# The last quarter of a feed-forward product as eight plain block products, and seven-product sums moved from GpSimd to VectorE

## The chip, the cores and the metric

The kernel runs on one core of a Trainium2 chip. The core has five engines, each with its own queue of instructions that it works off in order: TensorE (PE in the profile, with its weight loads as PEld), VectorE (DVE), ScalarE (ACT), GpSimd (POOL) and SyncE (SP), which here only issues DMAs. An instruction waits at the head of its queue for semaphores that other engines raise. The metric is the device time of one execution in microseconds (us): the median of three executions.

## The reference

One layer of a decoder block on 512 tokens of width 1024, all in float32. Three token mixers come first (sparse attention, block-sparse attention and a state-space scan), are gated, summed and projected. The change is in what follows them:

```python
h = rms_norm(x, norm2_g[l])
x = x + jnp.square(jax.nn.relu(h @ w_ff1[l])) @ w_ff2[l]      # w_ff1 1024x4096, w_ff2 4096x1024
```

## The kernel before

**Split products.** A float32 product is made of three passes on TensorE. Each operand is split into a high part (ScalarE writes a rounded copy) and a low part (operand minus high part, one subtraction). `mm3` (L358 to L361) issues high x high, high x low and low x high into one PSUM sum. So each operand tile costs one ScalarE activation and one subtraction before TensorE may use it.

**Weights.** `WS` (L120 and on) is a stream of weight blocks of 128x1024 elements. A block is loaded into a raw buffer (`wraw`, 3 buffers, DMA from SP's queue), split into `whi` on ScalarE (L158) and `wlo` on VectorE (L159), 6 buffers of each, and freed when TensorE has used it. `tick` splits up to three blocks past the one in use.

**The feed-forward stage.** The hidden 4096 columns are worked in four quarters q of 1024. `ff_up(q, m)` makes an eighth of a quarter of `h @ w_ff1`: 24 matmuls of 512 columns, then ReLU on ScalarE (L1404) and the square on VectorE (L1405) into tile `f` (`FA[q, half]`). `ff_down(q, i)` is one of the seven products of a fast 2x2 block scheme (seven block products in place of eight, at the price of block sums on both sides): 24 matmuls of 512 columns into two PSUM tiles `sc`, which VectorE then adds into the result `x2` or a partial sum `u2acc` (L1460). Three kinds of extra work belong to the scheme:

- the sums on the weights, in place in the blocks `qd` (L244 to L250), eight per quarter, on VectorE;
- the sums on the activations (L1420 to L1426, tile `fs` or in place in `f`), four per quarter, on GpSimd;
- the low part `fo` of each left operand (L1431), seven per quarter, on GpSimd; its high part `fh` is on ScalarE (L1430). `left(n)` does both, one product ahead.

In quarter 3, after product 2, `u2acc` is added into the three other parts of the result (L1463), one part on VectorE and two on GpSimd, and the parts are sent out as they are finished (L1466).

**Order.** `FSEQ` (L255 to L263) sets the order: the eight `ff_up` of quarter 0, then in each quarter the seven products, with the eight `ff_up` of the next quarter laid between them (1, 2, 1, 1, 1, 2, 0). Quarter 3 has nothing laid between. The tile scheduler then orders each engine's queue, with small moves about that order.

Of the kernel before, what the change touches and what calls it, by code (L numbers as in the profile page):

```python
# [8 lines left out]
F32R = mybir.dt.float32r  # L9
AF = mybir.ActivationFunctionType  # L10
ALU = mybir.AluOpType
# [4 lines left out]
D = 1024  # L16
D_IN = 11512
NB = 4
# [19 lines left out]
def build_kernel(ctx, tc, A, out):  # L38
    nc = tc.nc
    pe, act, dve, pool = nc.tensor, nc.scalar, nc.vector, nc.gpsimd  # L40
    done = set()

    def dram(ap, off, dims):
        return bass.AP(tensor=ap.tensor, offset=ap.offset + off, ap=dims)
# [4 lines left out]
    def f(ap):  # L49
        return ap.bitcast(F32)  # L50
# [3 lines left out]
    def popen(name, side="left", space=None, bufs=1):  # L54
        kw = dict(name=name, bufs=bufs, side=side)
        if space is not None:
            kw["space"] = space
            kw.pop("side")
        cm = tc.tile_pool(**kw)
        p = cm.__enter__()  # L60
        open_pools[name] = cm
        return p
# [26 lines left out]
    def ps(tag, shape, dt=F32, bufs=2):  # L89
        if tag == XT[0]:  # L90
            XT[1] += 1
            if XT[1] % 3 == 0:
                tag = "pF"
        return psp.tile(shape, dt, tag=tag, name=tag, bufs=PSB[tag])
# [88 lines left out]
    ws = WS()  # L183

    def wcols(w, ld, k0, nk, c0, n):
        return dram(w, k0 * 128 * ld + c0, [[ld, 128], [128 * ld, nk], [1, n]])
# [5 lines left out]
    def plan_ch(w, ld, c0, k0=0, nk=8):  # L192
        return ws.add([(wcols(w, ld, k0, nk, c0, 128), 128)], nk, 128)
# [32 lines left out]
    PROD = ("11", "t1", "t2", "t3", "22", "t4", "21")  # L226
    NEEDS = {"11": "11", "t1": "12", "t2": "22", "t4": "21"}

    def quad_block(q, i, s):
        name = PROD[i]  # L230

        def go(loading):
            if loading:
                nm = NEEDS.get(name)
                if nm:
                    t = FL[0].tile([128, 1024], F32, name=f"qd{nm}_{s}")
                    row, col = int(nm[0]) - 1, int(nm[1]) - 1
                    nc.sync.dma_start(t.rearrange("p (a b) -> p a b", b=512),
                                      wcols(A["w_ff2"], D, 8 * q + 4 * row + 2 * s, 2, 512 * col, 512))
                    QD[nm, s] = t  # L240
                return None
            b11, b12, b22, b21 = [QD.get((n, s)) for n in ("11", "12", "22", "21")]
            if name == "t1":
                dve.tensor_tensor(b11, b12, b11, op=ALU.subtract)  # L244
            elif name == "t2":
                dve.tensor_tensor(b11, b22, b11, op=ALU.subtract)
            elif name == "t3":
                dve.tensor_tensor(b12, b22, b12, op=ALU.subtract)
            elif name == "t4":
                dve.tensor_tensor(b11, b21, b11, op=ALU.subtract)  # L250
            return {"t3": b12, "22": b22, "21": b21}.get(name, b11)
        return ws.add(go, 2, 512)

    FL = [None]
    FSEQ = [("F", 0, m) for m in range(8)]  # L255
    for q in range(4):
        m = 0
        for i, nf in enumerate((1, 2, 1, 1, 1, 2, 0)):
            FSEQ.append(("G", q, i))
            for _ in range(nf):  # L260
                if q < 3:
                    FSEQ.append(("F", q + 1, m))
                    m += 1  # L263
    ff = {}
    for kind, q, i in FSEQ:
        if kind == "F":
            ff[kind, q, i] = plan_ch(A["w_ff1"], 4096, q * 1024 + 128 * i)
        else:
            ff[kind, q, i] = [quad_block(q, i, s) for s in range(2)]


    for t in range(1, NB):
# [39 lines left out]
    for t in range(NB):  # L312
# [4 lines left out]
        for k0 in range(0, KT, 4):  # L317
            p = ps("pT", [128, 4, 128])
# [23 lines left out]
    p = ps("pT", [128, 512])  # L342
# [15 lines left out]
    def mm3(o, lh, ll, rh, rl, first, last):  # L358
        pe.matmul(o, lh, rh, start=first, stop=False)  # L359
        pe.matmul(o, lh, rl, start=False, stop=False)  # L360
        pe.matmul(o, ll, rh, start=False, stop=last)  # L361
# [879 lines left out]
    def branches(ya):  # L1241
# [20 lines left out]
        for bi, br in enumerate(BR):  # L1262
# [31 lines left out]
            if br == "b1":  # L1294
# [4 lines left out]
                for half in range(2):  # L1299
                    for m in range(BH):  # L1300
                        wi = P["br_b1"][m]
                        wh, wl = ws.get(wi)
# [5 lines left out]
            for m in range(8):  # L1308
                load_g(8 * bi + m)
                load_g(8 * bi + m + 1)  # L1310
                th = th_.pop(8 * bi + m)
                if br[0] == "c":
                    dve.scalar_tensor_tensor(th, th, 1.0, R, op0=ALU.add, op1=ALU.mult)
                if m in pp:
                    p = pp.pop(m)
                else:
                    p = ps("pj", [128, 512])
# [21 lines left out]
        x2 = fp.tile([128, NB, D], F32, name="x2")  # L1339
# [37 lines left out]
        fl = FL[0] = popen("ffl")  # L1377
        U2 = fl.tile([128, 2, 512], F32, name="u2acc")
        FA = {}
        pp = {}  # L1380
        if NH:
            for m in range(NH):
                pp[m] = ps(("pj", "pj", "sc", "sc")[m], [128, 512])
            for half in range(2):
                cs = slice(256 * half, 256 * half + 256)
                for m in range(NH):
                    wh, wl = ws.get(ff["F", 0, m])
# [6 lines left out]
        def ff_up(q, m):  # L1394
            if m % 4 == 0:
                FA[q, m // 4] = fl.tile([128, 2, 4, 256], F32, name=f"f{m // 4}", bufs=2)
            if q == 0 and m in pp:
                p = pp.pop(m)
            else:
                p = ps("pj", [128, 512])  # L1400
                yield from proj_ch(ff["F", q, m], lambda i: h2h[:, i], lambda i: h2l[:, i], p)
            p2 = p.rearrange("p (a b) -> p a b", a=2)
            fq = FA[q, m // 4][:, :, m % 4]
            act.activation(fq, p2, AF.Relu)  # L1404
            dve.tensor_tensor(fq, fq, fq, op=ALU.mult)  # L1405


        ST, AO = {}, {}

        def left(n):  # L1410
            q, i = divmod(n, 7)
            if q > 3 or n in AO:
                return
            f1 = FA[q, 0]
            a11, a21 = f1[:, 0], f1[:, 1]
            if i not in (0, 3):
                a12, a22 = FA[q, 1][:, 0], FA[q, 1][:, 1]
            if i == 1:
                ST[0] = fl.tile([128, 4, 256], F32, name="fs")
                pool.tensor_tensor(ST[0], a21, a22, op=ALU.add)  # L1420
            elif i == 2:
                pool.tensor_tensor(ST[0], ST[0], a11, op=ALU.subtract)
            elif i == 3:
                pool.tensor_tensor(a21, a11, a21, op=ALU.subtract)
            elif i == 4:
                pool.tensor_tensor(ST[0], a12, ST[0], op=ALU.subtract)  # L1426
            src = a11 if i == 0 else a21 if i == 3 else a22 if i == 5 else a12 if i == 6 else ST[0]
            h_ = fl.tile([128, 4, 256], F32R, name="fh", bufs=2)
            l_ = fl.tile([128, 4, 256], F32R, name="fo", bufs=2)
            act.activation(h_, src, AF.Copy)  # L1430
            pool.tensor_tensor(l_, src, f(h_), op=ALU.subtract)  # L1431
            AO[n] = h_, l_

        def quad(h, n):
            return lambda tt: x2[:, 2 * h + tt, 512 * n:512 * n + 512]

        X11, X12, X21, X22 = quad(0, 0), quad(0, 1), quad(1, 0), quad(1, 1)
        UU = lambda tt: U2[:, tt]
        INTO = ((X11, UU), (X22, X12), (UU,), (X22, X21), (X12,), (X21,), (X11,))
        LAST = {3: (X22, 1, 1), 4: (X12, 0, 1), 5: (X21, 1, 0), 6: (X11, 0, 0)}  # L1440

        def ff_down(q, i):
            ah, al = AO.pop(7 * q + i)
            blk = [ws.get(b) for b in ff["G", q, i]]
            for tt in range(2):
                p = ps("sc", [128, 512])
                for j in range(4):
                    wh, wl = blk[j // 2]
                    cs = slice(128 * tt, 128 * tt + 128)
                    mm3(p, ah[:, j, cs], al[:, j, cs], wh[:, j % 2], wl[:, j % 2], j == 0, j == 3)  # L1450
                    if tt and j % 2:
                        ws.free(ff["G", q, i][j // 2])
                    if tt == 0 and j == 1:
                        left(7 * q + i + 1)
                    yield 3 * 213
                for d in INTO[i]:
                    if q == 0 and i == 0 and d is UU:
                        act.activation(d(tt), p, AF.Copy)
                    else:
                        dve.tensor_tensor(d(tt), d(tt), p, op=ALU.add)  # L1460
                if q == 3 and i == 2:
                    for d in (X22, X12, X21):
                        (dve if d is X22 else pool).tensor_tensor(d(tt), d(tt), UU(tt), op=ALU.add)  # L1463
                if q == 3 and i in LAST:
                    d, h, n = LAST[i]
                    nc.sync.dma_start(dram(out, (2 * h + tt) * 128 * D + n * 512, [[D, 128], [1, 512]]), d(tt))  # L1466

        for kind, q, i in FSEQ:
            if kind == "F":
                yield from ff_up(q, i)  # L1470
                if q == 0 and i == 5:
                    left(0)
            else:
                yield from ff_down(q, i)
        pclose("ffl")
        pclose("ff")

# [82 lines left out]
```

## Time and profile before

| what | value |
|---|---|
| median of three executions | 1436.81 us (1435.62 to 1438.63) |
| the profiled execution | 1434.21 us, its span in the trace 1432.5 us |
| PE busy | 1364.9 us, 95% of the span |
| DVE busy | 1089.1 us, 76% |
| ACT busy | 722.5 us, 50% |
| POOL busy | 482.4 us, 34% |
| feed-forward stage | about 1099 us to the end of the span |
| last quarter's products | from about 1377 us to the end |

Busy time of PE is time in which at least one matmul is under way; matmuls overlap, so what a matmul costs is read from the distance between two starts, not from its own duration. The profiled execution is 2.60 us under the median of the three, and its span leaves 1.71 us outside.

### The profile page before, as it was taken

What the parts mean: (1) busy time and instruction counts of PE and PEld (TensorE: products, weight loads), DVE (VectorE), ACT (ScalarE), POOL (GpSimd) and SP (SyncE); (2) the same over time, 40 slices, a digit from 0 to 9 for tenths busy, and PEclk for the clock granted to TensorE, in tenths of its full rate; (3) what the DMA queues carried; (4) which work ended last, traced back from release to release, by engine and by line L of the source; (5) the groups of instructions that cost most, each with busy time, mean ns of one, the idle gap of its engine ahead of it and who ended that gap; (6) DMA issues with size and microseconds to landing.
All of it is one profiled execution on the core that took longest, in us unless ns stands there. A gap on an engine that the chain in (4) does not pass through costs nothing.

```text
span 1432.5 us, 19782 instructions
## 1 busy us (share of the span) xinstructions
PE 1364.9 (95%) x6736; PEld 1121.9 (78%) x6736; DVE 1089.1 (76%) x1944; ACT 722.5 (50%) x1442; POOL 482.4 (34%) x342
## 2 busy tenths in 40 slices
PE   6989799999999989999999999999799999999988
PEld 5878688888887767888888777787589888888866
DVE  4599966898977555488568897888655797979796
ACT  5545236667665675555555555545324444444442
POOL 5455211101056676111013524424000342526265
PEclk9999899999999999999999999999899999999999
DMA  6336464453586688843337743424555232331401
GB/s 202 81 96 139 126 205 126 136 133 103 139 229 200 202 230 218 229 141 107 89 94 208 207 129 100 117 65 131 178 184 172 79 118 89 106 115 53 136 4 59
DMA packets 232098, 195.93 MB, mean 137 GB/s; under 512 B 17200, under 2 KB 183484, under 8 KB 231996
## 3 DMA queue, kind: packets, MB, share of 16 engines
q1 hardware_dynamic: 226524, 183.12, 44.3%
q0 software_dynamic: 4608, 8.39, 2.2%
q10 hardware_dynamic: 864, 3.15, 0.6%
q8 instruction: 53, 0.87, 0.3%
q14 instruction: 49, 0.40, 0.1%
HBM read 157.85 MB, written 36.77 MB: 136 GB/s over the span
## 4 chain that ended last, share of the span: by engine, by line
PE 70%; DVE 14%; DMA 7%; issue 4%; ACT 3%; POOL 2%; SPq 1%; DVEq 0%; POOLq 0%; ACTq 0%
PE pj L359 16%; PE pj L360 16%; PE pj L361 15%; PE sc L359 3%; PE sc L361 3%; PE sc L360 3%; PE pT L831 2%; DVE wlo L159 2%; PE sc L796 2%; PE sc L795 2%; PE pv L844 2%; PE pv L843 1%; DMA gld<-g_d 1%; DVE mask L766 1%; DMA E<-ac_d 1%
## 5 line engine op out<-in xcount | busy, mean ns | idle before, releaser
L158 ACT ACTIVATE whi<-wraw 128x1024 fp32r<-128x1024 f32 (+3 forms) x180 | 173.2, 971 | 176.3 <-PE pj L360 115.7
L159 DVE TENSOR_TENSOR wlo<-wraw,whi 128x1024 fp32r<-128x1024 f32 (+1 forms) x156 | 192.9, 1238 | 60.3 <-ACT whi L158 59.2
L359 PE MATMUL pj<-hTh,whi 128*128 128x512 f32 x384 | 154.9, 403 | 0.4 <-DVE cacc L726 0.4
L361 PE MATMUL pj<-hTh,wlo 128*128 128x512 f32 x384 | 153.6, 400 | 0.0
L360 PE MATMUL pj<-hTl,whi 128*128 128x512 f32 x384 | 153.3, 399 | 0.0
L359 PE MATMUL pj<-whi,hTh 128*128 128x512 f32 (+2 forms) x352 | 141.6, 404 | 8.3 <-DVE stk L429 3.1
L804 ACT ACTIVATE p<-p,nb,rs 128x256 f32<-128x256 f32 (+3 forms) x192 | 123.2, 645 | 52.0 <-DVE nb L802 52.0
L360 PE MATMUL pj<-wlo,hTh 128*128 128x512 f32 (+2 forms) x352 | 139.6, 397 | 0.1
L361 PE MATMUL pj<-whi,hTl 128*128 128x512 f32 (+2 forms) x352 | 138.3, 393 | 0.0
L159 DVE TENSOR_TENSOR wlo<-qd,whi 128x1024 fp32r<-128x1024 f32 x56 | 101.3, 1815 | 25.6 <-ACT whi L158 25.6
L359 PE MATMUL pj<-yh,whi 128*128 128x512 f32 x256 | 103.6, 409 | 9.8 <-ACT yh L709 8.2
L815 POOL TENSOR_TENSOR p<-p,rc 128x256 f32<-128x256 f32 (+3 forms) x48 | 38.2, 796 | 220.7 <-DVE rc L810 67.1
L158 ACT ACTIVATE whi<-qd 128x1024 fp32r<-128x1024 f32 x56 | 58.9, 1055 | 87.6 <-PE sc L361 38.9
L360 PE MATMUL pj<-yl,whi 128*128 128x512 f32 x256 | 102.6, 401 | 0.3 <-DVE yl L710 0.3
L361 PE MATMUL pj<-yh,wlo 128*128 128x512 f32 x256 | 102.3, 400 | 0.0
L359 PE MATMUL sc<-whi,fh 128*128 128x512 f32 x224 | 88.9, 397 | 8.2 <-DVE u2acc L1460 4.8
L360 PE MATMUL pj<-h2l,whi 128*128 128x512 f32 (+1 forms) x256 | 96.3, 376 | 0.0
L361 PE MATMUL pj<-h2h,wlo 128*128 128x512 f32 (+1 forms) x256 | 96.2, 376 | 0.0
L359 PE MATMUL pj<-h2h,whi 128*128 128x512 f32 (+1 forms) x256 | 96.1, 376 | 0.0
L360 PE MATMUL sc<-wlo,fh 128*128 128x512 f32 x224 | 88.6, 396 | 0.0
L361 PE MATMUL sc<-whi,fo 128*128 128x512 f32 x224 | 88.3, 395 | 0.0
L359 PEld LDWEIGHTS pj<-whi,hTh 128*128 128x128 f32 x352 | 68.2, 194 | 22.4 <-issue 6.6
(349 smaller groups left out, 3476.3 us busy)
## 6 DMA issues: line engine op xcount, KB each, us to landing
wraw<-in_w_in_dram SPq DMA_DIRECT2D x84, 512.0 KB, 4.4
wraw<-in_w_ff_dram SPq DMA_DIRECT2D x32, 512.0 KB, 4.3
qd<-in_w_ff_dram SPq DMA_DIRECT2D x32, 512.0 KB, 4.7
gld<-g_d SPq DMA_DIRECT2D x48, 256.0 KB, 3.2
q_d<-qev SPq DMA_DIRECT2D x128, 64.0 KB, 2.7
qu<-q_d POOLq DMA_DIRECT2D x32, 256.0 KB, 3.6
E<-ac_d SPq DMA_DIRECT2D x16, 512.0 KB, 4.9
wraw<-in_w_br_ssd_dram SPq DMA_DIRECT2D x16, 512.0 KB, 4.0
```

The lines of the kernel that those rows point to most:

```text
L158: act.activation(hi[:, :m], r[:, :m], AF.Copy)
L159: (pool if i < NP else dve).tensor_tensor(lo[:, :m], r[:, :m], f(hi[:, :m]), op=ALU.subtract)
L359: pe.matmul(o, lh, rh, start=first, stop=False)
L360: pe.matmul(o, lh, rl, start=False, stop=False)
L361: pe.matmul(o, ll, rh, start=False, stop=last)
L766: dve.scalar_tensor_tensor(wk, r[:, :n], iwt[:, b, h:h + 1], caus[:, 384 - 128 * b:] if h == 0 else wk, op0=ALU.mult, op1=ALU.add)
L795: pe.matmul(s_[:, h % w, :n], u.q[:, h], kh[:, :n], start=True, stop=False)
L796: pe.matmul(s_[:, h % w, :n], u.q[:, h], kl[:, :n], start=False, stop=True)
L804: act.activation(u.p[h][:, :n], u.p[h][:, :n], AF.Exp, bias=u.nb[:, h:h + 1], scale=rs8[:, u.b, u.h0 + h:u.h0 + h + 1], accum_out=u.sm[:, ...
L815: pool.tensor_tensor(u.p[h][:, :n], u.p[h][:, :n], bc(rc[:, h:h + 1], [128, n]), op=ALU.mult)
L831: pe.transpose(pt[:, h], u.p[h][:, kb * 128:kb * 128 + 128], ident)
L844: pe.matmul(o, vk, pl0, start=False, stop=en)
```

## The change

Two things. First, the sums on the activations, the low parts `fo`, and the additions of `u2acc` run on VectorE; GpSimd has no work left in the feed-forward stage. Second, quarter 3 is no longer seven products with sums but two plain products `ff_last(o)`, one for each half of the 1024 output columns: eight weight blocks `plain_block`, split in the ordinary way, four token tiles each of 24 matmuls in one PSUM sum `pj`. The left operands are the four quarters of `f` with no sums, `gh` and `gl` (high and low), made once and kept; they take the buffers of the weight blocks `qd` of the same shape. The additions of `u2acc` into the other parts move to quarter 2.

```diff
+    def plain_block(q, o, s):
+        ws_parts = [(wcols(A["w_ff2"], D, 8 * q + 2 * s, 2, 512 * o, 512), 512)]
+        return ws.add(ws_parts, 2, 512)
...
-    for q in range(4):
+    for q in range(3):
...
             for _ in range(nf):
-                if q < 3:
-                    FSEQ.append(("F", q + 1, m))
-                    m += 1
+                FSEQ.append(("F", q + 1, m))
+                m += 1
+    FSEQ += [("H", 3, 0), ("H", 3, 1)]
...
+        def ff_last(o):
+            if o == 0:
+                for nm, kh, th in (("12", 0, 0), ("22", 0, 1), ("11", 1, 0), ("21", 1, 1)):
+                    src = FA[3, kh][:, th]
+                    h_ = fl.tile([128, 4, 256], F32R, name=f"gh{nm}", tag=f"qd{nm}_0")
+                    l_ = fl.tile([128, 4, 256], F32R, name=f"gl{nm}", tag=f"qd{nm}_1")
+                    act.activation(h_, src, AF.Copy)
+                    dve.tensor_tensor(l_, src, f(h_), op=ALU.subtract)
+                    AO[kh, th] = h_, l_
+            idx = ff["H", 3, o]
+            for t in range(NB):
+                p = ps("pj", [128, 512])
+                cs = slice(128 * (t % 2), 128 * (t % 2) + 128)
+                for s in range(4):
+                    wh, wl = ws.get(idx[s])
+                    ah, al = AO[s // 2, t // 2]
+                    for k2 in range(2):
+                        j = 2 * (s % 2) + k2
+                        mm3(p, ah[:, j, cs], al[:, j, cs], wh[:, k2], wl[:, k2], s == 0 and k2 == 0, s == 3 and k2 == 1)
+                    if t == NB - 1:
+                        ws.free(idx[s])
+                    yield 6 * 213
+                x2s = x2[:, t, o * 512:o * 512 + 512]
+                dve.tensor_tensor(x2s, x2s, p, op=ALU.add)
+                nc.sync.dma_start(dram(out, t * 128 * D + o * 512, [[D, 128], [1, 512]]), x2s)
...
-                pool.tensor_tensor(ST[0], a21, a22, op=ALU.add)
+                dve.tensor_tensor(ST[0], a21, a22, op=ALU.add)
...
-            pool.tensor_tensor(l_, src, f(h_), op=ALU.subtract)
+            dve.tensor_tensor(l_, src, f(h_), op=ALU.subtract)
...
-                if q == 3 and i == 2:
+                if q == 2 and i == 2:
                     for d in (X22, X12, X21):
-                        (dve if d is X22 else pool).tensor_tensor(d(tt), d(tt), UU(tt), op=ALU.add)
-                if q == 3 and i in LAST:
-                    d, h, n = LAST[i]
-                    nc.sync.dma_start(dram(out, (2 * h + tt) * 128 * D + n * 512, [[D, 128], [1, 512]]), d(tt))
+                        dve.tensor_tensor(d(tt), d(tt), UU(tt), op=ALU.add)
```

The other three sums of `left` move from `pool` to `dve` in the same way. The order of every engine is the same before and after up to the feed-forward stage.

The first place is VectorE at the opening of quarter 2's products (about 1293 us in the trace of before). `f_12138` and `f_12407` are the two halves of quarter 2's activations, `qd` the weight blocks, `x` the result. Before:

```order
L246 TENSOR_TENSOR qd_0_12526<-qd_0_12726,qd_0_12526 128x1024
L1460 TENSOR_TENSOR x_10770<-x_10770,sc 128x512
L159 TENSOR_TENSOR wlo<-qd_1_12565,whi 128x1024
L1460 TENSOR_TENSOR x_10770<-x_10770,sc 128x512
L159 TENSOR_TENSOR wlo<-wraw,whi 128x1024
L246 TENSOR_TENSOR qd_1_12565<-qd_1_12758,qd_1_12565 128x1024
L1460 TENSOR_TENSOR x_10770<-x_10770,sc 128x512
```

After:

```order
L250 TENSOR_TENSOR qd_0_12526<-qd_0_12726,qd_0_12526 128x1024
L1491 TENSOR_TENSOR x_10770<-x_10770,sc 128x512
L1452 TENSOR_TENSOR fs<-f_12138,f_12407 128x1024
L159 TENSOR_TENSOR wlo<-qd_1_12565,whi 128x1024
L1491 TENSOR_TENSOR x_10770<-x_10770,sc 128x512
L1456 TENSOR_TENSOR f_12138<-f_12138 128x1024
L159 TENSOR_TENSOR wlo<-wraw,whi 128x1024
L250 TENSOR_TENSOR qd_1_12565<-qd_1_12758,qd_1_12565 128x1024
L1463 TENSOR_TENSOR fo<-fs,fh 128x1024
L1491 TENSOR_TENSOR x_10770<-x_10770,sc 128x512
```

Two sums and one low part, which stood in GpSimd's queue, now stand in VectorE's between the same seven instructions.

The second place is VectorE at the passage from quarter 2 to quarter 3 (about 1372 us). Before, the queue goes on with weight differences and low parts of `qd` blocks:

```order
L1405 TENSOR_TENSOR f_12988<-f_12988 128x2x256
L246 TENSOR_TENSOR qd_1_13146<-qd_1_13256,qd_1_13146 128x1024
L1460 TENSOR_TENSOR x_10770<-x_10770,sc 128x512
L159 TENSOR_TENSOR wlo<-qd_0_13107,whi 128x1024
L1460 TENSOR_TENSOR x_10770<-x_10770,sc 128x512
L159 TENSOR_TENSOR wlo<-qd_1_13146,whi 128x1024
L250 TENSOR_TENSOR qd_0_13107<-qd_0_13354,qd_0_13107 128x1024
L1460 TENSOR_TENSOR x_10770<-x_10770,sc 128x512
L1460 TENSOR_TENSOR u2acc<-u2acc,sc 128x512
```

After, with `gl` the low parts of quarter 3's activations, this is the rest of VectorE's queue to the end of the program:

```order
L159 TENSOR_TENSOR wlo<-wraw,whi 128x1024
L1411 TENSOR_TENSOR f_12994<-f_12994 128x2x256
L1491 TENSOR_TENSOR x_10770<-x_10770,sc 128x512
L1420 TENSOR_TENSOR gl_13262<-f_12994,gh_13261 128x1024
L1420 TENSOR_TENSOR gl_13266<-f_12994,gh_13265 128x1024
L1491 TENSOR_TENSOR x_10770<-x_10770,sc 128x512
L159 TENSOR_TENSOR wlo<-wraw,whi 128x1024 x2
L1436 TENSOR_TENSOR x_10770<-x_10770,pj 128x512 x3
L159 TENSOR_TENSOR wlo<-wraw,whi 128x1024 x2
L1436 TENSOR_TENSOR x_10770<-x_10770,pj 128x512 x5
```

What remains there is two low parts of activations, five of weights and eight additions of finished sums into the result.

## Rows read from the trace of the kernel before

**Rows 1.** Busy time by stretch: window, length, then PE, PEld, DVE, ACT, POOL busy (instructions), clock, DMA.
```profile
1254.00:1336.00 82.00, 82.00 (x364) 67.89 (x363) 69.32 (x59) 33.77 (x37) 31.66 (x11) 1.00 0.34 104
...
1372.00:1432.50 60.50, 48.60 (x194) 37.62 (x192) 47.25 (x41) 18.08 (x18) 39.00 (x14) 0.94 0.10 35
```

**Rows 2.** Waits of PE from 1099 us on: who for whom, total us, times, longest.
```profile
PE sc L359 <- DVE u2acc L1460: 4.8, 2, 4.3
...
PE sc L359 <- DVE x L1460: 3.4, 3, 2.7
```

**Rows 3.** Timeline of PE: start, us, engine, line, instruction [idle before, releaser].
```profile
1308.24 0.39 PE L359 MATMUL sc<-whi,fh 128*128 128x512 f32 x1
...
1363.77 0.39 PE L361 MATMUL pj<-h2h,wlo 128*128 128x512 f32 x1
...
1371.93 0.39 PE L361 MATMUL pj<-h2h,wlo 128*128 128x512 f32 x1
1372.16 0.39 PE L359 MATMUL sc<-whi,fh 128*128 128x512 f32 x1
...
1387.57 0.63 PE L359 MATMUL sc<-whi,fh 128*128 128x512 f32 x1 [4.31 <-DVE u2acc L1460]
1388.00 0.63 PE L360 MATMUL sc<-wlo,fh 128*128 128x512 f32 x1
...
1410.60 0.47 PE L359 MATMUL sc<-whi,fh 128*128 128x512 f32 x1 [2.70 <-DVE x L1460]
...
1428.42 0.39 PE L361 MATMUL sc<-whi,fo 128*128 128x512 f32 x1
```

**Rows 4.** Timeline of POOL, opening of quarter 2's products and of quarter 3's.
```profile
1300.21 3.37 POOL L1431 TENSOR_TENSOR fo<-fs,fh 128x1024 fp32r<-128x1024 f32 x1
...
1381.81 3.34 POOL L1431 TENSOR_TENSOR fo<-fs,fh 128x1024 fp32r<-128x1024 f32 x1
```

**Rows 5.** Timeline of DVE, the same two places and the last addition.
```profile
1286.53 1.21 DVE L244 TENSOR_TENSOR qd<-qd,qd 128x1024 f32<-128x1024 f32 x1
1287.66 1.21 DVE L159 TENSOR_TENSOR wlo<-wraw,whi 128x1024 fp32r<-128x1024 f32 x1
...
1293.42 1.22 DVE L246 TENSOR_TENSOR qd<-qd,qd 128x1024 f32<-128x1024 f32 x1
...
1301.26 3.42 DVE L246 TENSOR_TENSOR qd<-qd,qd 128x1024 f32<-128x1024 f32 x1
1304.59 0.68 DVE L1460 TENSOR_TENSOR x<-x,sc 128x512 f32<-128x512 f32 x1
1305.19 0.67 DVE L1460 TENSOR_TENSOR u2acc<-u2acc,sc 128x512 f32<-128x512 f32 x1
...
1382.86 3.37 DVE L250 TENSOR_TENSOR qd<-qd,qd 128x1024 f32<-128x1024 f32 x1
...
1428.84 0.69 DVE L1460 TENSOR_TENSOR x<-x,sc 128x512 f32<-128x512 f32 x1 [2.03 <-PE sc L361]
```

**Rows 6.** DVE by groups from 1372 us on: count, busy us, mean ns, idle before.
```profile
L159 DVE TENSOR_TENSOR wlo<-qd,whi 128x1024 fp32r<-128x1024 f32 x11 | 24.2, 2200 | 0.8 <-ACT whi L158 0.8
```

**Rows 7.** Timeline of ACT, opening of quarter 2's products and the passage to quarter 3.
```profile
1294.89 1.06 ACT L158 ACTIVATE whi<-qd 128x1024 fp32r<-128x1024 f32 x1 [2.76 <-issue]
1296.25 1.06 ACT L158 ACTIVATE whi<-wraw 128x1024 fp32r<-128x1024 f32 x1 [0.29 <-PE sc L361]
1297.21 1.05 ACT L1430 ACTIVATE fh<-fs 128x1024 fp32r<-128x1024 f32 x1
...
1372.18 1.06 ACT L158 ACTIVATE whi<-qd 128x1024 fp32r<-128x1024 f32 x1 [3.89 <-PE pj L360]
1373.14 0.58 ACT L1404 ACTIVATE f<-pj 128x512 f32<-128x512 f32 x1
```

**Rows 8.** DMA issues by line: count, size each, median us to landing.
```profile
qd<-in_w_ff_dram SPq DMA_DIRECT2D x32, 512.0 KB, 4.7
```

**Rows 9.** Busy time of the opening of quarter 2's products, columns as in rows 1.
```profile
1293.42:1321.14 27.72, 27.72 (x124) 22.95 (x123) 26.97 (x20) 12.21 (x13) 22.04 (x7) 1.00 0.14 38
```

More of the change, by code (lines that the diff above doesn't have):

```diff
@@ L267, in build_kernel @@
             ff[kind, q, i] = plan_ch(A["w_ff1"], 4096, q * 1024 + 128 * i)
+        elif kind == "G":
+            ff[kind, q, i] = [quad_block(q, i, s) for s in range(2)]
         else:
-            ff[kind, q, i] = [quad_block(q, i, s) for s in range(2)]
+            ff[kind, q, i] = [plain_block(q, i, s) for s in range(4)]
     for t in range(1, NB):
@@ L1411, in left @@
             q, i = divmod(n, 7)
-            if q > 3 or n in AO:
+            if q > 2 or n in AO:
                 return
@@ L1419, in left @@
                 ST[0] = fl.tile([128, 4, 256], F32, name="fs")
-                pool.tensor_tensor(ST[0], a21, a22, op=ALU.add)
+                dve.tensor_tensor(ST[0], a21, a22, op=ALU.add)
             elif i == 2:
-                pool.tensor_tensor(ST[0], ST[0], a11, op=ALU.subtract)
+                dve.tensor_tensor(ST[0], ST[0], a11, op=ALU.subtract)
             elif i == 3:
-                pool.tensor_tensor(a21, a11, a21, op=ALU.subtract)
+                dve.tensor_tensor(a21, a11, a21, op=ALU.subtract)
             elif i == 4:
-                pool.tensor_tensor(ST[0], a12, ST[0], op=ALU.subtract)
+                dve.tensor_tensor(ST[0], a12, ST[0], op=ALU.subtract)
             src = a11 if i == 0 else a21 if i == 3 else a22 if i == 5 else a12 if i == 6 else ST[0]
@@ L1439, in branches @@
         INTO = ((X11, UU), (X22, X12), (UU,), (X22, X21), (X12,), (X21,), (X11,))
-        LAST = {3: (X22, 1, 1), 4: (X12, 0, 1), 5: (X21, 1, 0), 6: (X11, 0, 0)}
         def ff_down(q, i):
@@ L1472, in branches @@
                     left(0)
+            elif kind == "G":
+                yield from ff_down(q, i)
             else:
-                yield from ff_down(q, i)
+                yield from ff_last(i)
         pclose("ffl")
```

## The prediction

> **What bounds the kernel now.** I read the busy time by stretch first. In quarter 2's stretch TensorE is busy for all of 82.00 us at clock 1.00; in the last 60.50 us it is busy for 48.60 us and the clock is 0.94 [rows 1]. So the feed-forward stage has two parts with different limits. The waits of TensorE confirm it: from 1099 us on it has five waits that count, all before products `sc`, all on VectorE's additions, 8.2 us together [rows 2], and the timeline of TensorE puts them in quarter 3 [rows 3]. Before that, TensorE alone sets the time, and nothing done on VectorE or GpSimd can make it shorter, only longer.
>
> What a matmul of 512 columns costs at full clock is the distance of two starts: 1363.77 to 1371.93 us is 36 of them, 0.2267 us each [rows 3]. From 1372.16 us (first matmul of the last product of quarter 2) to the last matmul at 1428.42 us there are 192 matmuls, 24 of that product and 7 x 24 of quarter 3. Their starts would span 191 x 0.2267 = 43.30 us; they span 56.26 us. So **quarter 3 loses 12.96 us** on TensorE. Part of it is waiting (one wait alone is 4.31 us), part the slow clock behind a wait: after the wait that ends at 1387.57 the distance is 0.43 us, the 1.2 GHz level [rows 3].
>
> Why only there: in quarters 0 to 2 the eight `ff_up` blocks, 8 x 24 x 0.2267 = 43.5 us of TensorE, lie between the products and give VectorE and GpSimd time. In quarter 3 there are none, while each product still wants its weight sums, weight lows and additions on VectorE and its sum and low part on GpSimd, one after the other.
>
> A second thing is in the rows. A VectorE operation with 1024 columns and both inputs in SBUF takes 1.21 us, start to start 1.13 us, when GpSimd is quiet (1286.53 to 1287.66), and 3.42 or 3.37 us when GpSimd is at work (1301.26 beside the low part of 1300.21; 1382.86 beside that of 1381.81). The additions from PSUM, 512 columns, take 0.68 us beside either, 0.60 start to start [rows 4, 5]. In quarter 3 the weight lows average 2.20 us [rows 6]. **Each of the two engines slows the other**, and GpSimd's own operation takes 3.3 to 3.4 us.
>
> **The change, part by part.**
>
> *Quarter 3's matmuls.* Seven products of 24 become eight blocks' worth: two halves x four token tiles x 24 = 192 matmuls for 168. TensorE gets 24 x 0.2267 = **5.44 us more work**. Shapes and operand types are the same, so the same price holds.
>
> *Quarter 3's side work.* Gone are 8 weight sums, 6 of 14 weight splits, the 4 activation sums, 3 of 7 activation splits, and of 20 additions into `x2` and `u2acc` all but 8. What is left at the passage is short. The last `ff_up` ends at 1372.16. ScalarE makes one weight high part (to 1373.24) and the last ReLU (to 1373.72) [rows 7]; VectorE the low part of that block (about 1374.5), the square (0.68, about 1375.1); then ScalarE the two high parts `gh` (1.06 each, start to start about 1.0 [rows 7]: to 1377.2), and VectorE an addition and the two `gl` (1.21 each: the first at about 1377.4, the second 1378.6). TensorE is meanwhile in the last product of quarter 2, until 1372.16 + 24 x 0.2267 = 1377.60, and the first plain sum starts with 12 matmuls on the other half of the activations, done long before. `gh` and `gl` are first wanted at 1377.60 + 2.72 = 1380.32: **2.7 us or more to spare**, and the scheduler has also put matmuls of the next sum there. If the cover fails, the delay is what exceeds 2.7 us.
>
> *Its weights.* Blocks 0 to 3 take the places in the split buffers that the first blocks of quarter 3 take now, so they are split as early as those. Blocks 6 and 7 take the buffers of blocks 0 and 1, free after the 78th and 84th matmul, at 1395.3 and 1396.6; a high and a low part are 1.06 + 1.21, so both are there by about 1399.2, and the second half starts at 1377.60 + 96 x 0.2267 = 1399.36 and wants block 6 at its 13th matmul, 1402.1. Bytes loaded are the same, eight blocks of 512 KB. I take nothing for this; the bound is one late block, its load of 4.7 us [rows 8] + 1.06 + 1.21 = 7 us once.
>
> *Its outputs.* Eight as before, the last after the last addition. The tail from the last matmul's start to the end of the span is 1432.5 - 1428.42 = 4.08 us and stays.
>
> *Sums and lows on VectorE in quarters 0 to 2.* Eleven operations per quarter move, 11 x 1.13 = 12.4 us. VectorE is busy 69.32 of 82 us there, but at the long durations. At the quiet ones a quarter has 22 weight lows and 8 weight sums (30 x 1.13) and 8 squares and 20 additions (28 x 0.60): 50.7 us, with the eleven 63.1, 77% of 82. The opening of a quarter's products is the dense place: VectorE is busy 26.97 of 27.72 us [rows 9]. That is 9 operations of 1024 columns and 9 of 512 whole; the new order puts 6 more of 1024 into the same piece. At quiet prices 15 x 1.13 + 9 x 0.60 = 22.4 us: it fits, with 5.3 us over.
>
> Now the waits that this adds: a low part now waits at the head of VectorE's queue for ScalarE's `fh`, and behind it stand the additions that free PSUM and the next weight lows, for which TensorE waits. I follow the second piece of the order from 1293.42 [rows 5]: weight sum, addition (1294.55), activation sum (1295.15), weight low (1296.28; its high part is there at 1295.95), addition (1297.42), activation sum (1298.02), weight low (1299.15; high part at 1297.31), weight sum (1300.29), low part `fo` (1301.42; `fh` was done at 1298.26 in the order of now) to 1302.63; the times of the high parts are in [rows 7]. On GpSimd it ended at 1300.21 + 3.37 = 1303.58 [rows 4], and TensorE starts that product at 1308.24 [rows 3]. So the low part comes about 1 us **earlier** than now, and 5.6 us before its product. I take nothing for the quarters' openings, with 0 to some 2 us each as the bound.
>
> *The six additions of `u2acc` in quarter 2.* Three of 512 columns, 3 x 0.60 = 1.8 us, twice, about 1326 and 1332 us. Behind them stand weight lows of the product after next, and an `ff_up` (5.4 us) lies between each two products there. Nothing for the sum; 1.8 us each if the cover were gone.
>
> VectorE's 1024-column operations take 1.21 us beside a quiet GpSimd and 3.37 us beside a busy one [rows 5]. A rule of the Trainium skill speaks against the move: Trace Analysis, section Optimizing Scalar/DVE Operations, says that where VectorE is saturated it may make sense to give work to ScalarE or even GpSimd, and here work is given back to it. The same paragraph adds that the two share an SBUF read port, so that moving work between them might not help, and SBUF — State Buffer, section Who interferes with whom, says that a VectorE instruction with two SBUF inputs contends with a GpSimd instruction that reads SBUF. By the first sentence alone the openings overflow (the third rival's sum); by the second the 3.37 us go back to 1.21. The trace agrees with the second: 1.21 against 3.37 us.
>
> *Sum.* From 1372.16 there are 24 + 192 = 216 matmuls without a wait; the last starts at 1372.16 + 215 x 0.2267 = 1420.90, 7.52 us earlier than 1428.42. (12.96 of loss gone, 5.44 of work added.) The profiled execution was 1434.21, so 1426.69 in its terms; it lies 2.60 under the median of the three, 1436.81. Against that median: 1436.81 - 7.5 = **1429.3 us**.
>
> **The rivals.**
>
> 1. *A smaller gain*: openings and passage cost TensorE 1 to 4 us in all, since the scheduler's order was made for other durations and VectorE holds more in one queue. For it: the dense stretch [rows 9] and the one queue. Against: 5 us to spare where I followed it. 1430.3 to 1433.3.
>
> 2. *The change doesn't remove the wait but moves it to the weights*: one plain block is late at the head of a half, 7 us once. For it: the plain stage runs through four blocks in its first 24 matmuls, 5.4 us, where a product used two. Against: the blocks ahead of it are split while TensorE is in earlier work. 1429.3 + 7 = 1436.3, no change.
>
> 3. *VectorE becomes the bound, and it is slower*: the long durations do not come from GpSimd, but from something that stays, such as ScalarE or the DMAs. Then the opening of each quarter gets six more operations of 2.20 us [rows 6], 13.2 us on top of 26.97 in 27.72 us; 12.5 over, less some 5 us of slack before the product that waits, 7.5 us each, three times: 1429.3 + 22 = 1452 us. It decides from the mean duration at which 15 x d + 9 x 0.60 fills 27.72 us: d = 1.49 us. Against it: every long row that I saw lies beside a GpSimd row, and the quiet 1.21 us rows have ScalarE and DMA at work beside them.
>
> **How the numbers follow.** Forecast 0.80; rival 1 0.09; rival 2 0.06; rival 3 0.05. A difference of 0.2%, 2.9 us, is about what a measurement of this kernel can tell from no change. The forecast and nearly all of rival 1 lie beyond it: faster 0.88, same 0.07, slower 0.05. The range takes the forecast with the spread of the three runs (1.2 below their median, 1.8 above), some more below for that median's own error, and rival 1 but for its end: 1426.8 to 1432.8.
>
> **What would show it.** TensorE at clock 1.00 and without a wait over 1 us from 1099 us to the end; 192 matmuls into `pj` in some 43.5 us, the last starting near 1420.9; VectorE's 1024-column operations all near 1.2 us in the stage, its busy time per quarter near 63 us; GpSimd empty. Wrong would be: waits of TensorE on `fo`, `wlo` or on additions at about 1140, 1215 or 1297 us (rivals 1 and 3), on `whi` or a load at about 1378 or 1400 us (rival 2), or 1024-column operations over 1.5 us with GpSimd idle (rival 3).

## The result

The changed kernel takes **1427.97 us**, median of 5 runs (1425.82 to 1431.64); the kernel before, run beside it, 1438.56 us (5 runs, 1435.62 to 1441.98). The ratio on record is **0.9948, with a 95% interval of 0.9927 to 0.9969**: faster by 0.5%. It is not the quotient of these two medians, which is 0.9926; e0 below, against 18 runs of the kernel before, has 0.9948 too. The forecast was 1429.3 us in a range of 1426.8 to 1432.8.

The profiled execution took 1425.82 us with a span of 1424.1 us. Busy time of the page of after, share of the span and number of instructions for each engine:

```profile
PE 1365.5 (96%) x6760; PEld 1126.1 (79%) x6760; DVE 1044.6 (73%) x1959; ACT 712.6 (50%) x1433; POOL 347.0 (24%) x294
```

Busy time of after by stretch, columns as in [rows 1]; the second line is the stretch of quarter 2, the third the last part of the kernel, the fourth the opening of quarter 2's products as in [rows 9]:

```profile
1172.00:1254.00 82.00, 82.00 (x364) 67.89 (x363) 64.98 (x71) 33.74 (x37) 0.00 (x0) 1.00 0.34 103
1254.00:1336.00 82.00, 82.00 (x364) 67.89 (x363) 68.60 (x76) 33.75 (x37) 0.00 (x0) 1.00 0.26 77
1372.00:1424.10 52.10, 48.44 (x214) 39.79 (x212) 15.70 (x18) 6.87 (x8) 0.00 (x0) 0.99 0.17 61
1293.42:1321.14 27.72, 27.72 (x124) 22.96 (x123) 27.20 (x30) 12.19 (x13) 0.00 (x0) 1.00 0.20 57
```

GpSimd (the last busy column) is empty. From 1372 us on VectorE has 18 operations instead of 41, and the clock is 0.99 instead of 0.94. The waits of TensorE from 1095 us on had two groups that counted [rows 2]; after, that view has no row at all.

TensorE's timeline of after, at the places of [rows 3]: start, duration, engine, line, instruction.

```profile
1307.86 0.39 PE L365 MATMUL sc<-whi,fh 128*128 128x512 f32 x1
...
1371.32 0.39 PE L365 MATMUL sc<-whi,fh 128*128 128x512 f32 x1
...
1376.76 0.39 PE L365 MATMUL pj<-whi,gh 128*128 128x512 f32 x1
...
1420.06 0.39 PE L367 MATMUL pj<-whi,gl 128*128 128x512 f32 x1
```

The second and the last row are what the forecast was made of: from the first matmul of quarter 2's last product to the last matmul of the kernel, 1371.32 to 1420.06, it takes **48.74 us** where it took 56.26. The forecast's sum says 215 x 0.2267 = 48.74. Of the 8.4 us by which the profiled span became shorter (1432.5 to 1424.1), 7.5 are these; 0.84 come from ahead of the change: the first matmul of the last stage's `ff_up` starts at 1085.39 instead of 1086.23, in code that is the same in both. That matmul in the two timelines, before and after:

```profile
1086.23 0.28 PE L359 MATMUL pj<-h2h,whi 128*128 128x256 f32 x1
```

```profile
1085.39 0.28 PE L365 MATMUL pj<-h2h,whi 128*128 128x256 f32 x1
```

### The profile page after: what moved, and what is told of

It is laid out like the page before. It is cut to its first block, busy times and chain, and to the rows that moved or that the text cites. A ratio compares the mean times of both kernels' runs of the same rounds, so it can differ in the third digit from the quotient of the medians.

```text
span 1424.1 us, 19720 instructions
## 1 busy us (share of the span) xinstructions
PE 1365.5 (96%) x6760; PEld 1126.1 (79%) x6760; DVE 1044.6 (73%) x1959; ACT 712.6 (50%) x1433; POOL 347.0 (24%) x294
## 4 chain that ended last, share of the span: by engine, by line
PE 71%; DVE 10%; DMA 7%; issue 4%; ACT 4%; POOL 2%; SPq 2%; DVEq 0%; ACTq 0%; POOLq 0%
PE pj L365 17%; PE pj L366 17%; PE pj L367 16%; PE sc L366 3%; PE sc L367 3%; PE sc L365 3%; PE pT L837 2%; PE sc L802 2%; PE sc L801 2%; PE pv L850 2%; PE pv L849 2%; DVE wlo L159 1%; DMA gld<-g_d 1%; SPq L525 1%; DMA E<-ac_d 1%
## 5 line engine op out<-in xcount | busy, mean ns | idle before, releaser
L158 ACT ACTIVATE whi<-wraw 128x1024 fp32r<-128x1024 f32 (+3 forms) x188 | 181.7, 975 | 210.8 <-PE pj L366 124.3
L365 PEld LDWEIGHTS pj<-hTh,whi 128*128 128x128 f32 x384 | 72.3, 188 | 16.4 <-issue 1.7
L367 PEld LDWEIGHTS pj<-hTh,wlo 128*128 128x128 f32 x384 | 72.2, 188 | 15.2 <-issue 1.2
L366 PEld LDWEIGHTS pj<-hTl,whi 128*128 128x128 f32 x384 | 72.3, 188 | 15.0 <-issue 1.7
L841 ACT ACTIVATE pth<-pT 128x512 fp32r<-128x512 f32 x95 | 55.0, 593 | 56.8 <-PE pT L837 54.8
L366 PEld LDWEIGHTS pj<-wlo,hTh 128*128 128x128 f32 x352 | 68.4, 194 | 14.9 <-issue 2.2
```

Of the source, the lines that this page charges most:

```text
L158: act.activation(hi[:, :m], r[:, :m], AF.Copy)
L841: act.activation(ph, ptf, AF.Copy)
```

## The experiments

Since the part ahead of the feed-forward stage does not take the same time twice, I compare two stretches inside the profiled execution: **A**, from the first `ff_up` matmul (`pj` from `h2h`) to the first matmul of quarter 2's last product; and **B**, from there to the last matmul. Before: A 285.93 us, B 56.26 us. B is 43.30 us for seven products without any loss and 48.74 us for eight blocks. A and B are read from one profiled execution of each kernel; e3 to e7 also have one run each, so their whole times tell little.

| kernel | first `ff_up` starts at | A | B | loss in B | time, us (runs) |
|---|---|---|---|---|---|
| before | 1086.23 | 285.93 | 56.26 | 12.96 | 1438.56 (5) |
| the change | 1085.39 | 285.93 | 48.74 | 0.0 | 1427.97 (5) |
| e0_change | 1085.17 | 285.93 | 48.73 | 0.0 | 1427.35 (6) |
| e1_plain_only | 1082.11 | 285.93 | 48.73 | 0.0 | 1427.10 (7) |
| e2_move_only | 1087.79 | 285.93 | 54.76 | 11.46 | 1433.83 (12) |
| e3_lows_twice | 1086.96 | 285.93 | 48.73 | 0.0 | 1427.4 (1) |
| e4_lows_four | 1086.69 | 309.62 | 48.73 | 0.0 | 1450.82 (1) |
| e5_24_fewer | 1093.75 | 285.93 | 43.30 | 0.0 | 1428.74 (1) |
| e6_fewer_adds | 1088.84 | 285.93 | 47.68 | 4.38 | 1428.26 (1) |
| e7_four_psum | 1092.23 | 285.93 | 51.90 | 8.60 | 1435.83 (1) |

e0, e1, e2 and e5 ran on one chip, where the kernel before took 1435.35 us (18 runs); e3, e4, e6 and e7 on another, 1434.82 us (1 run).

### Which part of the change does it: e0, e1, e2

**e0_change** is the changed kernel again, for the comparison on one chip.

> The changed kernel again, beside the others of this call. Theory: 0.9948 of the kernel before, about 7.5 us less, from quarter 3 alone; from the last product of quarter 2 on, 216 matmuls of 0.2267 us without a wait, the last start 48.7 us after the first.

Measured: 1427.35 us, ratio 0.9948 (0.9928 to 0.9968), B 48.73 us.

**e1_plain_only** keeps the plain quarter 3 and puts the sums and low halves of the activations back on GpSimd (one line of five shown):

```diff
-            dve.tensor_tensor(l_, src, f(h_), op=ALU.subtract)
+            pool.tensor_tensor(l_, src, f(h_), op=ALU.subtract)
```

> Only one part of the change: quarter 3 as plain products, but the sums and low parts of quarters 0 to 2 stay on GpSimd. Theory (TensorE is the bound in quarters 0 to 2 whatever the other two engines do, and the plain products alone end quarter 3's waits): 7.5 us less than before, no wait of TensorE from 1099 us on, while VectorE's operations with 1024 columns still take 2 to 3.4 us beside GpSimd. Rival (the gain needs the move to VectorE, since the slow operations hold up the passage to quarter 3): less than 4 us gained, with waits of TensorE at about 1297 or 1377 us.

Measured: 1427.10 us, ratio 0.9952 (0.9933 to 0.9970), B 48.73 us, A 285.93 us, and no wait row of TensorE from 1095 us on. **The plain quarter 3 alone is the whole gain.** The move is worth nothing in quarters 0 to 2, though it does change VectorE's durations. Groups of VectorE from 1172 to 1372 us (count, busy us, mean ns of one, idle before them), first after, then e1:

```profile
L159 DVE TENSOR_TENSOR wlo<-qd,whi 128x1024 fp32r<-128x1024 f32 x32 | 38.9, 1221 | 18.5 <-ACT whi L158 18.5
L159 DVE TENSOR_TENSOR wlo<-wraw,whi 128x1024 fp32r<-128x1024 f32 x22 | 26.9, 1224 | 24.6 <-ACT whi L158 24.6
L1491 DVE TENSOR_TENSOR x<-x,sc 128x512 f32<-128x512 f32 x40 | 26.5, 682 | 0.2
```

```profile
L159 DVE TENSOR_TENSOR wlo<-qd,whi 128x1024 fp32r<-128x1024 f32 x32 | 56.6, 1779 | 16.3 <-ACT whi L158 16.3
L159 DVE TENSOR_TENSOR wlo<-wraw,whi 128x1024 fp32r<-128x1024 f32 x22 | 32.1, 1457 | 18.1 <-ACT whi L158 18.1
L1491 DVE TENSOR_TENSOR x<-x,sc 128x512 f32<-128x512 f32 x39 | 25.8, 679 | 0.2
```

With GpSimd at work the low parts of the summed weight blocks take 1.78 us on average, without it 1.22; the additions from PSUM take 0.68 us either way. These are the durations that the Trainium skill (SBUF — State Buffer, section Who interferes with whom) would lead one to look for: it says that a VectorE instruction contends with a reading GpSimd instruction when both its inputs lie in SBUF, and not with at most one there, outside VectorE's two-port modes; the trace agrees. But all of it is hidden behind TensorE, which is busy for the whole of both stretches.

**e2_move_only** is the kernel before, with seven products in quarter 3, and everything that GpSimd did in this stage on VectorE:

```diff
-            pool.tensor_tensor(l_, src, f(h_), op=ALU.subtract)
+            dve.tensor_tensor(l_, src, f(h_), op=ALU.subtract)
...
-                        (dve if d is X22 else pool).tensor_tensor(d(tt), d(tt), UU(tt), op=ALU.add)
+                        dve.tensor_tensor(d(tt), d(tt), UU(tt), op=ALU.add)
```

> Only the other part: the sums, low parts and additions of the partial sum on VectorE, quarter 3 still as seven products. At quiet prices VectorE has from 1372 us on 25 operations of 1.13 us and 29 of 0.60 us, 45.7 us, against 43.3 us of TensorE for its 192 matmuls. Theory (the two engines slow each other, so quarter 3's loss is mostly their collision): the loss of 12.96 us falls to 3 to 6 us, 7 to 10 us less than before, as good as the whole change. Rival (the one queue of VectorE is as slow as the two engines side by side, and only the plain products help): the loss stays over 10 us, less than 3 us gained.

Measured: 1433.83 us, ratio 0.9991 (0.9976 to 1.0005), B 54.76 us: a loss of 11.46 us where my theory had 3 to 6. The whole time does not differ from the kernel before beyond its interval. **My theory fell**, and the rival was right: one queue of VectorE with all the work is nearly as slow as the two engines side by side. TensorE's waits of e2 from 1095 us on:

```profile
PE sc L359 <- DVE u2acc L1460: 3.5, 2, 2.4
PE sc L359 <- DVE x L1460: 3.1, 1, 3.1
PE sc L361 <- DVE fo L1431: 0.3, 1, 0.3
```

VectorE's timeline of e2 in quarter 3:

```profile
1383.46 1.22 DVE L250 TENSOR_TENSOR qd<-qd,qd 128x1024 f32<-128x1024 f32 x1
1384.59 1.22 DVE L1431 TENSOR_TENSOR fo<-fs,fh 128x1024 fp32r<-128x1024 f32 x1
...
1413.03 1.22 DVE L159 TENSOR_TENSOR wlo<-qd,whi 128x1024 fp32r<-128x1024 f32 x1
1414.16 1.35 DVE L1460 TENSOR_TENSOR x<-x,sc 128x512 f32<-128x512 f32 x2
1418.03 0.69 DVE L1460 TENSOR_TENSOR x<-x,sc 128x512 f32<-128x512 f32 x1 [2.52 <-PE sc L361]
```

Busy time of e2 from 1373.72 us, where B starts, to 1415.50, and over the whole of B; then over B in the kernel before (columns as in [rows 1]):

```profile
1373.72:1415.50 41.78, 34.79 (x135) 26.79 (x134) 41.23 (x48) 16.79 (x17) 0.00 (x0) 0.92 0.04 13
1373.72:1428.48 54.76, 47.77 (x192) 37.49 (x191) 45.22 (x53) 17.85 (x18) 0.00 (x0) 0.94 0.09 34
```

```profile
1372.16:1428.42 56.26, 48.05 (x193) 37.49 (x191) 46.40 (x40) 18.08 (x18) 39.00 (x14) 0.94 0.09 33
```

The durations are the quiet ones, 1.22 us where they were 3.37 [rows 5], and yet VectorE is busy for 41.23 of 41.78 us. Over B it is busy 45.22 us with 53 operations, against 46.40 us with 40 operations before: the operations that came from GpSimd took up what the shorter durations gave. VectorE is the bound of this stretch in both kernels. Only after 1415.50 does it wait for TensorE, and there more than two products are still to be multiplied, 12.98 us up to 1428.48.

This does not show that the two engines cost each other little in the kernel before. There, two groups of VectorE hold the long operations of quarter 3, the low parts of [rows 6] and two weight sums (from 1372.16 us on):

```profile
L250 DVE TENSOR_TENSOR qd<-qd,qd 128x1024 f32<-128x1024 f32 x2 | 5.5, 2775 | 0.0
```

At 1.21 us each the two groups would take 24.2 - 13.3 = 10.9 and 5.5 - 2.4 = 3.1 us less, 14.0 us of VectorE's time. The move takes these away, and brings ten operations of 1.13 us and four of 0.60 us into B, 13.7 us. By this estimate it is an even trade. A run without the collision and without the added work was not made.

The trace of before also shows what the collision is. From 1099 us on, 37 of the 38 VectorE operations of 1024 columns that took over 1.3 us (rows of one operation alone) end 1.08 to 1.10 us after the GpSimd operation that was running when they began, whether they began early in it or late; the 38th ran beside two GpSimd additions that the trace merges into one row. So VectorE's operation in effect waits until GpSimd's is done. In [rows 4, 5] GpSimd is done at 1385.15 and VectorE at 1386.23. GpSimd's next operation is done at 1388.44, and VectorE's, though it began 2.12 us into it, at 1389.53. The last row is a GpSimd operation with VectorE idle for most of it; it takes 2.40 us where the one of [rows 4] beside VectorE's takes 3.34.

```profile
1385.23 3.21 POOL L1422 TENSOR_TENSOR fs<-fs,f 128x1024 f32<-128x1024 f32 x1
```

```profile
1387.35 2.18 DVE L250 TENSOR_TENSOR qd<-qd,qd 128x1024 f32<-128x1024 f32 x1
```

```profile
1418.94 2.40 POOL L1431 TENSOR_TENSOR fo<-f,fh 128x1024 fp32r<-128x1024 f32 x1 [3.99 <-ACT fh L1430]
```

### What kind of limit quarter 3 had: e6, e7

Both start from e2. **e6_fewer_adds** leaves out additions of quarter 3:

```diff
-                for d in INTO[i]:
+                for d in (INTO[i][:1] if q == 3 else INTO[i]):
...
-                if q == 3 and i == 2:
+                if q == 3 and i == 2 and False:
```

> The move alone (quarter 3 as seven products, all side work on VectorE), with 12 additions of quarter 3 left out, so that part of the result is missing: the second target of the three products that have two, and the six additions of the partial sum. They stand in VectorE's queue but prepare no operand: 12 x 0.60 = 7.2 us. From the first matmul of quarter 2's last product to the last matmul it was 54.76 us with them, 11.46 over the 43.30 of TensorE. Theory (quarter 3 is held by the amount of work in VectorE's one queue): 47 to 50 us. Rival (it is held by the chain sum, high part, low part, product, whose length the additions do not change): 53 us or more.

Measured: B 47.68 us. 12 additions of 0.60 us, 7.2 us of VectorE's queue, take **7.08 us** off the end, and the rival's 53 us is not reached. So in e2 it is in the main the sum of what stands in VectorE's queue that set quarter 3's end, not one chain of dependent steps. Busy time of e6 over B, and VectorE's last weight low part:

```profile
1374.77:1422.45 47.68, 44.47 (x192) 35.46 (x191) 38.11 (x41) 17.85 (x18) 0.00 (x0) 1.00 0.11 39
```

```profile
1409.16 1.22 DVE L159 TENSOR_TENSOR wlo<-qd,whi 128x1024 fp32r<-128x1024 f32 x1
```

The two figures agree more closely than their parts. That low part starts 39.31 us after the start of B in e2 and 34.39 us in e6, 4.92 us sooner; the other 2.16 us lie behind it, and TensorE's clock over B is 1.00 here and 0.94 in e2. Six of the twelve additions also read a PSUM buffer, which comes free sooner without them; e6 does not part this from the queue.

**e7_four_psum** gives quarter 3's products four PSUM buffers instead of two:

```diff
-                p = ps("sc", [128, 512])
+                p = ps("pj" if q == 3 and i % 2 else "sc", [128, 512])
```

> The move alone, with quarter 3's products in turn in the two PSUM buffers `sc` and the two of `pj` that lie idle there, so that TensorE need not wait for an addition before the next product. TensorE's waits in the move alone are named after these additions. Theory (the queue of VectorE is what is full, the PSUM wait only where it shows): 52 us or more from the first matmul of quarter 2's last product to the last, little under the 54.76. Rival (two PSUM buffers are too few): 48 us or less, a version that beats the change.

Measured: B 51.90 us, 2.86 us of the 11.46 won, between the two bounds that were set for it: a little under the theory's 52 us, far over the rival's 48. TensorE's waits of e7 from 1095 us on:

```profile
PE sc L359 <- ACT fh L1430: 2.1, 1, 2.1
PE sc L361 <- DVE fo L1431: 1.5, 1, 1.5
PE pj L359 <- DVE x L1460: 1.5, 1, 1.5
```

The waits for additions are shorter, and waits for the activations' halves have come in their place: a part of the loss was buffers. That the rest is VectorE's queue fits e2 and e6, but e7 does not show it by itself. Of the versions with seven products and all their additions this is the best, and it still needs 3.17 us more for B than eight plain blocks.

### Is TensorE the bound now: e5

**e5_24_fewer** leaves 24 of the 192 matmuls of quarter 3 out, the number by which eight blocks exceed seven products:

```diff
-                    for k2 in range(2):
+                    for k2 in range(1 if s == 3 else 2):
```

> The change with 24 of the 192 matmuls of the plain products left out (the last eighth of the inner dimension of each sum), so that part of the result is not computed. Theory (TensorE sets the end, 0.2267 us a matmul): from the first matmul of quarter 2's last product to the last matmul 191 x 0.2267 = 43.3 us, 5.4 us less than the change. Rival (weights, loads or VectorE set the pace of the plain stage): less than 3 us shorter, with waits of TensorE in its place.

Measured: B 43.30 us, which is 5.43 us less: 24 x 0.2267 = 5.44. TensorE alone sets the end of the changed kernel, and the price of the added work is what the forecast took. The whole time, 1428.74 us, shows nothing of that: in this execution the first `ff_up` started 8.4 us later than in the change, ahead of everything edited. TensorE's timeline of e5:

```profile
1379.68 0.39 PE L365 MATMUL sc<-whi,fh 128*128 128x512 f32 x1
```

```profile
1422.98 0.39 PE L367 MATMUL pj<-whi,gl 128*128 128x512 f32 x1
```

### How much room VectorE has in quarters 0 to 2: e3, e4

The changed kernel, with each low half of quarters 0 to 2's products made two and four times over (7 and 21 operations more in each quarter):

```diff
-            dve.tensor_tensor(l_, src, f(h_), op=ALU.subtract)
+            for _ in range(2):
+                dve.tensor_tensor(l_, src, f(h_), op=ALU.subtract)
```

> The change with the low part of each left operand of quarters 0 to 2 made twice on VectorE, the same result written again: 7 more operations of 1.13 us per quarter, 2 or 3 of them in the dense opening. Theory (the opening fits with 5.3 us over in 27.7): still no wait of TensorE over 1 us from 1099 us on, and the last matmul 48.7 us after the first matmul of quarter 2's last product. Rival (VectorE's queue was already at its end, as its busy share of 27.2 of 27.7 us in the opening suggests): 3 us or more of waits in each of three openings, 9 us or more.

> The change with each of these low parts made four times: 21 more operations of 1.13 us per quarter, so 63.1 + 23.7 = 86.8 us of VectorE in a quarter's 81.6 us of TensorE. Theory (VectorE becomes the bound where its work at quiet prices exceeds TensorE's): waits of TensorE in each of the three quarters, some 5 us each and more in the openings, 10 to 25 us in all over the change. Rival (TensorE is covered by far more than the sum says): under 5 us.

Measured: e3 is free, A 285.93 us and no wait row; e4 costs 23.7 us in A. Busy time of e3 in quarter 1's stretch and in the opening of quarter 2's products:

```profile
1172.00:1254.00 82.00, 82.00 (x363) 67.89 (x363) 72.32 (x76) 34.39 (x38) 0.00 (x0) 1.00 0.34 105
...
1293.00:1321.00 28.00, 28.00 (x126) 23.17 (x125) 27.48 (x31) 12.45 (x13) 0.00 (x0) 1.00 0.15 44
```

e4, stretches of quarters 1 and 2, and its three largest waits of TensorE from 1095 us on:

```profile
1172.00:1254.00 82.00, 78.48 (x338) 62.46 (x336) 80.18 (x82) 32.53 (x36) 0.00 (x0) 1.00 0.28 88
1254.00:1336.00 82.00, 75.22 (x317) 59.95 (x318) 77.34 (x80) 28.36 (x32) 0.00 (x0) 0.98 0.29 90
```

```profile
PE sc L367 <- DVE fo L1464: 7.5, 5, 3.2
PE pj L367 <- DVE wlo L159: 3.9, 3, 3.3
PE pj L365 <- ACT whi L158: 2.3, 2, 1.3
```

Where A ends in e4, 1086.69 + 309.62 us:

```profile
1396.31 0.39 PE L365 MATMUL sc<-whi,fh 128*128 128x512 f32 x1
```

The room is between 7 and 21 operations per quarter. In e3 the dense opening shows 98% for VectorE and TensorE loses nothing. That VectorE is full over a short stretch does not say that it is late: it fills such a stretch with operations that are wanted later. Over a whole quarter the share tells more; in quarter 1's stretch it is 65 of 82 us in the change, 72 in e3 and no wait, 80 in e4 and waits.

## Why the prediction was right, step by step

- *The loss of quarter 3, 12.96 us, goes.* Right: B is 48.74 us in the change, e0, e1 and e3, which is 215 distances of 0.2267 us with no loss left.
- *5.44 us more matmul work.* Right: e5 takes it out again and gains 5.43.
- *The sum.* It put the last matmul at 1420.90; it started at 1420.06, and the 0.84 us between them had arisen ahead of the stage. 48.74 us from the first `sc` were forecast, and 48.74 measured. That the whole time lies only 1.3 us from the forecast is in part luck: the forecast went out from a median of 1436.81 us, the runs beside the change have 1438.56, and the medians differ by 10.6 us here and by 8.0 in e0, where the stretch accounts for 7.52.
- *What caused the loss.* Here the prediction had two reasons side by side: too little time for side work, because no `ff_up` block lies between the products, and the slowing of VectorE and GpSimd by each other. Both are real: in e2 and e6 the sum of VectorE's work sets the pace without any collision, and in the kernel before the collision takes up 14 us of VectorE's time by the estimate above. How the 12.96 us divide between them no run shows, since the move takes the second away and adds to the first; it gives 1.5 us back. The forecast did not depend on the split, since the plain quarter 3 does away with both; my expectation for e2 did, and failed. It set 45.7 us of VectorE against 43.3 us of TensorE as if the two could overlap to the end, but 12.98 us of matmuls were left when VectorE's full stretch was over: 41.78 + 12.98 = 54.76.
- *The passage is covered.* Right, with room. The forecast had the first `gl` done at 1377.4, the second at 1378.6, and the first use of the pair at 1380.32: 2.9 and 1.7 us to spare. Its 2.7 us is the length of the 12 matmuls before that use. VectorE's timeline of after at the passage, and at the second half of quarter 3:

```profile
1372.39 1.23 DVE L159 TENSOR_TENSOR wlo<-wraw,whi 128x1024 fp32r<-128x1024 f32 x1 [3.61 <-ACT whi L158]
...
1375.34 2.36 DVE L1420 TENSOR_TENSOR gl<-f,gh 128x1024 fp32r<-128x1024 f32 x2 [0.41 <-ACT gh L1419]
...
1395.79 2.58 DVE L159 TENSOR_TENSOR wlo<-wraw,whi 128x1024 fp32r<-128x1024 f32 x2 [1.82 <-ACT whi L158]
...
1420.48 0.69 DVE L1436 TENSOR_TENSOR x<-x,pj 128x512 f32<-128x512 f32 x1 [4.75 <-PE pj L367]
```

  The second row holds both `gl`, done at 1377.70, which is 1378.54 with the 0.84 us added that the stage started earlier.
- *Blocks 6 and 7 come in time.* Right: ScalarE starts block 6's high part at 1394.69 (forecast 1395.3, or 1394.5 with the 0.84 taken off), both low parts are done at 1398.37 in the third row above, and no wait follows. ScalarE's row:

```profile
1394.69 1.06 ACT L158 ACTIVATE whi<-wraw 128x1024 fp32r<-128x1024 f32 x1 [16.54 <-PE pj L367]
```

- *The openings hold.* Right. The low part that I followed through the queue was forecast to start at 1301.42, with the 0.84 us 1300.58; VectorE's timeline of after has it at 1300.59:

```profile
1292.58 1.22 DVE L250 TENSOR_TENSOR qd<-qd,qd 128x1024 f32<-128x1024 f32 x1
1294.32 1.22 DVE L1452 TENSOR_TENSOR fs<-f,f 128x1024 f32<-128x1024 f32 x1
...
1300.59 1.22 DVE L1463 TENSOR_TENSOR fo<-fs,fh 128x1024 fp32r<-128x1024 f32 x1
```

  Wrong was the reason of the other estimate, 22.4 us of work in 27.72: VectorE is busy for 27.20 us of it, with 30 operations. The order has more than these operations ready, and VectorE simply goes on with them; e3 shows that the slack is there all the same.
- *VectorE's busy time per quarter.* 63.1 us forecast, 64.98 measured in quarter 1's stretch, and 68.60 in quarter 2's, where the six additions of `u2acc` stand as well.
- *The move is worth nothing in the sum.* Right: e1 without it and e0 with it have the same A and B, and times of 1427.10 and 1427.35 us. In this case it is worth nothing where TensorE is the bound and 1.5 us of B where VectorE is. The Trainium skill (Perfetto Trace Analysis, section Optimizing Scalar/DVE Operations) leaves open whether moving work between VectorE and GpSimd helps.
- *The rivals.* None took place: no wait on `fo`, `wlo`, `whi` or an addition in the stage (rivals 1 and 2), no 1024-column operation of more than 1.3 us in the rows shown with GpSimd idle (rival 3). e4 shows what the third would have looked like: waits on `fo` and `wlo`, and 23.7 us.

## What to carry to other kernels

Before an arithmetic saving is counted, add up per stretch what it puts on the engines that prepare its operands and collect its sums: seven products instead of eight save TensorE 5.44 us, and in a stretch without other matmul work they cost it 12.96 us here, so by these prices the saving pays in quarters 0 to 2, where TensorE does not wait, and not in the last. Moving work from one of two engines that hold each other up to the other is no test of what the collision costs (e2): it takes the collision away and adds the work, and VectorE's busy time in B went only from 46.4 to 45.2 us. Whether the sum in one queue sets the end is told by taking out a known part of it (e6). And a full engine in a short window is no bound as long as nothing waits for it; doubling a part of its work tells.

## What the runs showed of the hardware

- The stage is steadier than the run. In nine of ten kernels A is 285.93 us, equal to 0.01 us, while its start varies from 1082.11 to 1093.75 us, in code that none of the edits touched. So in these profiled executions the spread of several us lies ahead of this stage; some of it in waits for loads (`pT` for `bcx` from `BC_d`: 6.0 us before, 3.6 in e1, 8.1 in e2). What varies there I did not look into.
- A loss on a wait has a second part. In e2 the waits in B add up to 6.9 us, the loss is 11.46. The granted clock goes with a part of the rest: it is 0.92 in the stretch where TensorE waits (first window of e2), 0.99 from 1372 us on in the change, where it does not. It is not all of it: in e6, at 1.00 over B, the waits add up to 3.2 us and the loss is 4.38.
- VectorE's operation of 1024 columns with both inputs in SBUF ends 1.08 to 1.10 us after GpSimd's, where it began beside one (37 of 38 in the stage of before); its addition from PSUM takes 0.68 us either way. GpSimd too takes longer beside VectorE: its low part of 1024 columns takes 3.3 to 3.4 us in [rows 4] and 2.40 us at 1418.94, where VectorE has one addition from PSUM beside it. The same operation on VectorE takes 1.22 us.
